# Attention products in halves, squares on ScalarE, tanh gates and a modulation plan in a two-layer encoder kernel

## The chip, the cores and the metric

The kernel runs as one program on one core of a Trainium2 chip. The metric is the device time of one execution in microseconds (us). Five engines matter: PE (TensorE, the matrix multiplier, with its weight loads listed as PEld), DVE (VectorE), ACT (ScalarE), POOL (GpSimd) and SP (SyncE, which here only issues transfers). Each engine takes its own instructions strictly in the order in which they stand; an instruction that waits holds up all behind it on its engine.

## The reference

Two layers, 256 tokens of width 2048, everything in float32. Each layer has an attention part and a feed-forward part, both behind a modulated norm:

```
mod = silu(c) @ ada_w[l] + ada_b[l]            # 6 rows of 2048: shifts, scales, gates
h   = rmsnorm(x) * (1 + sc_a) + sh_a
qa, ka, va, qb, kb, vb, ga, gb = split_cols(h @ w_in[l])
ya  = window_attention(rotary(norm(qa)), rotary(norm(ka)), va, sink) @ w_proj_a   # 8 heads, 2 of k and v
yb  = neighbourhood_attention(norm(qb), norm(kb), vb, bias) @ w_proj_b            # 8 heads
x   = x + gt_a * ((sigmoid(ga) * ya + sigmoid(gb) * yb) @ w_out)
h   = rmsnorm(x) * (1 + sc_m) + sh_m
g, v = split(conv3(h @ w_up))                  # 2 x 5632
x   = x + gt_m * ((silu(g) * v) @ w_down)
```

`norm` of q and k is an RMS norm over the 128 columns of a head. Attention is softmax(q k^T + mask or bias) v in both branches; branch A also has one sink logit per head in the softmax's sum.

## The kernel before, in words

**Products in halves.** A float32 matrix product is made of three products of the reduced type float32r. An operand is split into a high half (`hi`, a cast by ACT) and what is left over (`lo`, a subtraction by DVE), and PE adds hi·hi, hi·lo and lo·hi in PSUM. All weights go this way. They come in *units* of 16 blocks of 128x128 (1 MB, tile `w`), 232 units a layer, in the order in which PE needs them. For each unit ACT casts two halves of 128x1024 (`hl`, L296) and DVE subtracts (L297). There are four buffers for raw megabytes (weights `w` and modulation rows `aw` share them) and four for halves, so two units lie split ahead of PE. `features` multiplies activations of 256 tokens by a block (L313 to L315, 256 columns each); `tokens` makes rows of q, k and v (L373 to L375, 512 columns each).

**Attention before.** Only the products inside attention are done in plain float32: the scores `sc` (L570: two matmuls a head) and the outputs `po` (L601: two matmuls a head). The trace shows each float32 matmul as two records. Between them stand the mask with the row maximum (DVE, L574), the exponential (ACT, L582), the scaling (ACT, L590), four transposes (PE, `tp`, L595) and a copy of their result to SBUF (ACT, `pT`, L597). A head's output is itself split (`oA`, `oB`, L603 and L604). The heads run in a background job, several steps a unit (`ATT`), so their instructions lie between the weights' products.

**Norm of q and k** (`qk_rows`): for each of two token tiles ACT squares all heads' columns at once (L525), DVE sums each head's 128 columns (L526), a few small steps and a power on POOL (L420) give the factors, DVE multiplies (L534), and PE turns the result (`qtp`, L558).

**Gates.** Branch A's gate is `ya` (L864, in the second layer's start L735), branch B's is `gb` (L889), both a sigmoid on ACT. DVE multiplies the projected branches by them (L875 and L901) and the sum is split for the next product (L903).

**Modulation** (`ada`). Each of 96 columns of 128 values a layer is one transfer of 1 MB and one long DVE reduction (L225). In the first layer, while the first q, k and v groups are made, a job (`job0`) alternates two such reductions with one chunk of `h` (L445, L448, L449); its pace is `FIRST_RATE`, steps a unit. Afterwards `ADA_PLAN_0` and `ADA_PLAN_1` say how many reductions are done by which unit.

**Order.** The program text gives instructions priorities; a list scheduler that works with its own costs then fixes the order on each engine. All transfers are issued by SP in one order.

## Time and profile before

| | |
|---|---|
| three timed runs | 2687.84, 2690.78 (median), 2696.68 us |
| the profiled execution | 2687.88 us; its span on the core 2686.1 us, so 1.8 us lie around the span |
| busy: PE, DVE, ACT | 2663.7, 2086.4, 1402.2 us |
| transfers | 700 MB, 70.9% of the 16 DMA engines' time |

A busy PE is PE with a matmul in flight; matmuls overlap, so the mean duration of one (276 to 283 ns for 256 columns) is longer than the distance between two starts. Distances are therefore read from starts, or from a count of matmuls in a stretch where PE never idles. "Granted clock" (PEclk) is the share of full speed at which PE may run.

### The profile page before, as it was taken

The page shows a single profiled execution, that of the slowest core. Times are in us where ns is not written, and L with a number is a line of the kernel's source. Part 1 is how long each engine was busy: PE and PEld are TensorE (multiplying, and loading weights), DVE is VectorE, ACT ScalarE, POOL GpSimd, SP SyncE. Part 2 cuts the span into 40 slices and gives each one's busy share as a digit, 9 for nine tenths or more (in the row PEclk, how much of TensorE's full clock was granted, in tenths as well). Part 3 has the DMA queues.
Part 4 walks back from the last instruction along what each step waited for, and adds up shares of the span by engine and source line. Part 5 has one row for each costly group of instructions (what it writes and reads, how often), then busy time and mean ns, then how long its engine had stood idle before and what let it go on. Part 6 is the DMA issues. An engine that isn't in the chain of part 4 may idle for free.

```text
span 2686.1 us, 50251 instructions
## 1 busy us (share of the span) xinstructions
PE 2663.7 (99%) x21128; PEld 2568.6 (96%) x21128; DVE 2086.4 (78%) x2909; ACT 1402.2 (52%) x2077; POOL 33.8 (1%) x25
## 2 busy tenths in 40 slices
PE   8999999999999999999999999999999999999999
PEld 6988799999999999999998889999999999999999
DVE  7998997897987888788886666658878866665664
ACT  4434674455653555355564556544565445544553
POOL 0000100000000000000000000000000000000000
PEclk9999999999999999999999999999999999999999
DMA  8987688886788888778756656676747765555554
GB/s 345 348 330 280 242 300 328 332 313 221 282 288 291 294 290 295 297 285 295 288 213 243 249 210 226 224 265 254 291 171 289 295 252 191 197 193 191 194 197 142
DMA packets 102036, 700.38 MB, mean 261 GB/s; under 512 B 12721, under 2 KB 15025, under 8 KB 17969
## 3 DMA queue, kind: packets, MB, share of 16 engines
q1 hardware_dynamic: 101810, 697.17, 70.9%
q8 instruction: 165, 2.70, 0.4%
q14 instruction: 61, 0.50, 0.0%
HBM read 695.03 MB, written 2.10 MB: 260 GB/s over the span
## 4 chain that ended last, share of the span: by engine, by line
PE 88%; DVE 6%; DMA 3%; issue 2%; ACT 1%; POOL 1%; DVEq 0%; ACTq 0%; POOLq 0%
PE ps L313 24%; PE ps L315 24%; PE ps L314 24%; PE ps_t L374 4%; PE ps_t L375 4%; PE ps_t L373 4%; DMA aw<-in_aw 3%; DVE hl L297 2%; DVE aw L225 1%; PE po L601 1%; PE sc L570 1%; ACT hl L296 1%; POOL qrs L420 1%; PE tp L595 1%; DVE qn L534 0%
## 5 line engine op out<-in xcount | busy, mean ns | idle before, releaser
L297 DVE TENSOR_TENSOR hl<-w,hl 128x1024 fp32r<-128x1024 f32 x928 | 1129.5, 1223 | 366.6 <-ACT hl L296 364.8
L296 ACT CAST hl<-w 128x1024 fp32r<-128x1024 f32 x928 | 970.5, 1049 | 737.1 <-PE ps L315 478.0
L313 PE MATMUL ps<-h,hl 128*128 128x256 f32 x3328 | 923.3, 278 | 0.2 <-ACT hl L296 0.2
L314 PE MATMUL ps<-h,hl 128*128 128x256 f32 x3328 | 920.0, 277 | 0.0
L315 PE MATMUL ps<-h,hl 128*128 128x256 f32 x3328 | 919.8, 277 | 0.0
L313 PEld LDWEIGHTS ps<-h,hl 128*128 128x128 f32 x3328 | 624.8, 188 | 1.2 <-ACT hl L296 0.6
L314 PEld LDWEIGHTS ps<-h,hl 128*128 128x128 f32 x3328 | 625.3, 188 | 0.4
L315 PEld LDWEIGHTS ps<-h,hl 128*128 128x128 f32 x3328 | 624.3, 188 | 0.1
L225 DVE CUSTOM_DVE_ANT_0 aw<-aw,cact,ab 128x2048 f32<-128x2048 f32 x189 | 443.8, 2349 | 61.7 <-DMA aw<-in_aw 60.9
L373 PE MATMUL ps_t<-hl,h 128*128 128x512 f32 x576 | 227.2, 398 | 6.9 <-ACT h L448 3.6
L374 PE MATMUL ps_t<-hl,h 128*128 128x512 f32 x576 | 226.7, 394 | 0.9 <-DVE hl L297 0.8
L375 PE MATMUL ps_t<-hl,h 128*128 128x512 f32 x576 | 226.2, 394 | 0.0
L937 DVE SCALAR_TENSOR_TENSOR u<-ps,cw,u 128x255 f32<-128x255 f32 x304 | 146.4, 482 | 67.5 <-ACT u L935 63.5
L935 ACT ACTIVATE u<-ps,cw 128x256 f32<-128x256 f32 x152 | 85.7, 564 | 179.2 <-PE ps L315 179.1
L315 PE MATMUL ps<-merged,hl 128*128 128x256 f32 x512 | 142.0, 278 | 0.4 <-DVE hl L297 0.4
L313 PE MATMUL ps<-merged,hl 128*128 128x256 f32 x512 | 141.8, 278 | 0.5 <-DVE m L901 0.5
L314 PE MATMUL ps<-merged,hl 128*128 128x256 f32 x512 | 141.8, 277 | 0.0
L314 PE MATMUL ps<-act_o,hl 128*128 128x256 f32 x512 | 141.4, 276 | 0.0
L315 PE MATMUL ps<-act_o,hl 128*128 128x256 f32 x512 | 141.3, 276 | 0.0
L313 PE MATMUL ps<-act_o,hl 128*128 128x256 f32 x512 | 141.2, 276 | 0.0
L373 PEld LDWEIGHTS ps_t<-hl,h 128*128 128x128 f32 x576 | 108.8, 189 | 31.0 <-ACT h L448 4.6
L374 PEld LDWEIGHTS ps_t<-hl,h 128*128 128x128 f32 x576 | 109.2, 190 | 24.5 <-DVE hl L297 1.9
(215 smaller groups left out, 4562.2 us busy)
## 6 DMA issues: line engine op xcount, KB each, us to landing
w<-in_ws SPq DMA_DIRECT2D x463, 1024.0 KB, 5.0
aw<-in_aw SPq DMA_DIRECT2D x189, 1024.0 KB, 6.0
bias<-in_bias SPq DMA_DIRECT2D x16, 256.0 KB, 5.1
x<-in_xT SPq DMA_DIRECT2D x4, 512.0 KB, 5.3
aw_o<-in_aw SPq DMA_DIRECT2D x2, 1024.0 KB, 12.7
out<-x SPq DMA_DIRECT2D x16, 128.0 KB, 2.6
w<-in_ws SPq DMA_DIRECT2D x2, 512.0 KB, 12.1
aw_b<-in_aw SPq DMA_DIRECT2D x1, 1024.0 KB, 17.4
```

What stands on the lines that cost most here:

```text
L225: nc.vector.tensor_tensor_reduce(out=raw[:], in0=raw[:], in1=cact[:], scale=1.0, scalar=ab[:, i : i + 1], op0=ALU.mult, op1=ALU.add, accum ...
L296: nc.scalar.copy(hl[:, 0], r)
L297: nc.vector.tensor_tensor(out=hl[:, 1], in0=r, in1=hl[:, 0].bitcast(F32), op=ALU.subtract)
L313: nc.tensor.matmul(out, hi, act[0], start=first, stop=False)
L314: nc.tensor.matmul(ps[:, :S], hi, act[1], start=False, stop=False)
L315: nc.tensor.matmul(out, lo, act[0], start=False, stop=last)
L373: nc.tensor.matmul(ps[:], xh, hi, start=kc == kcs[0], stop=False)
L374: nc.tensor.matmul(ps[:], xh, lo, start=False, stop=False)
L375: nc.tensor.matmul(ps[:], xl, hi, start=False, stop=kc == kcs[-1])
L420: nc.gpsimd.tensor_tensor(out=dst, in0=src, in1=mhalf[:, :k], op=ALU.pow)
L935: nc.scalar.activation(out=u, in_=ps, func=AF.Identity, scale=w[:, 1:2], bias=w[:, 3:4])
L937: nc.vector.scalar_tensor_tensor(out=u[:, to], in0=ps[:, of], scalar=w[:, j : j + 1], in1=u[:, to], op0=ALU.mult, op1=ALU.add)
```

## The change

Six things are done together.

1. `attend` takes its operands as tuples. Where an operand comes as (hi, lo), the product is made of three float32r products (`by`). The outputs `po` go this way in both layers, the scores only in the second (`SCORES_3 = (1,)`). For this `pT` is split as it leaves PSUM (ACT cast and DVE subtraction of 512 columns in place of one ACT copy), v is split once per key head (2 in branch A, 8 in branch B), and in the second layer q (16), kA (2) and kB (8) are split too, 256 columns each.
2. `qk_rows`: ACT squares each head's 128 columns apart and sums them itself (`accum_out`), 52 instructions a layer in place of 14; the DVE sums L526 are gone.
3. Gates: sigmoid(z) = (1 + tanh(z/2)) / 2. ACT computes the tanh (same count of instructions); DVE multiplies by (1 + t) with one three-operand instruction in place of a product, and the factor 1/2 goes into the split of the merged sum.
4. The first layer's job follows `FIRST_PLAN`, steps done by a unit on straight lines, in place of rates.
5. Sixteen small matmuls of no use (`warm(WARM_ROW)`) stand behind the first chunk's products.
6. Buffers: the bias of branch B lands in the tile `p` itself; the small per-layer tables have one buffer in place of two, so the second layer's load later; sizes of fill-ins are adjusted.

```diff
-FIRST_RATE = [1.2, 1.0, 1.0]
+FIRST_PLAN = [(0, 6), (10, 17), (42, 48)]
+WARM_ROW = 16
+SCORES_3 = (1,)
...
+            if self.l == 0:
+                while ran[0] < on_line(FIRST_PLAN, self.u, True):
+                    first_step()
...
+                if self.l == 0 and self.u == 1 and self.at == 4:
+                    warm(WARM_ROW)
...
+        nc.scalar.activation(out=dst[:, 0], in_=src, func=AF.Copy, scale=scale)
+        nc.vector.scalar_tensor_tensor(
+            out=dst[:, 1], in0=src, scalar=scale, in1=dst[:, 0].bitcast(F32), op0=ALU.mult, op1=ALU.subtract
+        )
+    def half_tanh(dst, src, **kw):
+        nc.scalar.activation(out=dst, in_=src, func=AF.Tanh, scale=0.5, **kw)
+    def gated(dst, half, src):
+        nc.vector.scalar_tensor_tensor(out=dst, in0=half, scalar=1.0, in1=src, op0=ALU.add, op1=ALU.mult)
...
-            sq = at.tile([P, 512], F32, name="qsq", tag="qsq", bufs=1)
-            nc.scalar.activation(out=sq[:, :n], in_=ps[:, cols : cols + n], func=AF.Square)
-            nc.vector.tensor_reduce(
-                out=ss[:, t * heads : (t + 1) * heads], in_=sq[:, :n].rearrange("p (h d) -> p h d", d=HEAD), axis=AX.X, op=ALU.add
-            )
+            for i in range(heads):
+                sq = at.tile([P, HEAD], F32, name="qsq", tag="qsq", bufs=1)
+                nc.scalar.activation(
+                    out=sq[:], in_=ps[:, cols + i * HEAD : cols + (i + 1) * HEAD], func=AF.Square,
+                    accum_out=ss[:, t * heads + i : t * heads + i + 1],
+                )
...
+    def by(x):
+        return ((0, 0), (0, 1), (1, 0))[: 2 * len(x) - 1]
...
-            nc.tensor.matmul(sc[:, t], qT[:, t * P : (t + 1) * P], kT, start=True, stop=True)
+            for i, j in by(q):
+                nc.tensor.matmul(sc[:, t], q[i][:, t * P : (t + 1) * P], k[j], start=i + j == 0, stop=(i, j) == by(q)[-1])
...
-        pT = at.tile([P, 2, S], F32, name="pT", tag="pT", bufs=1)
-        nc.scalar.copy(pT[:], tp[:])
+        pT = at.tile([P, 2, 2, S], F32R, name="pT", tag="pT", bufs=1)
+        split(pT, tp[:])
...
-        for k in range(2):
-            nc.tensor.matmul(po[:, :S], v(k), pT[:, k], start=k == 0, stop=k == 1)
+        for i, j in by(v):
+            for b in range(2):
+                nc.tensor.matmul(po[:, :S], v[i][:, b], pT[:, j, b], start=i + j + b == 0, stop=i + b == 2)
...
-            bias = at.tile([P, 2, S], F32, name="bias", tag="bias", bufs=1)
-            nc.sync.dma_start(bias[:], a["bias"][l, hb])
+            p = at.tile([P, 2, S], F32, name="p", tag="p")
+            nc.sync.dma_start(p[:], a["bias"][l, hb])
...
-                split(merged[mo], z[:])
+                split(merged[mo], z[:], 0.5)
```

How the order moves is shown at three places. In its rows the numbers behind a name are layer-internal buffer numbers; `hl_2_0` is the first half of unit 2.

**DVE near the start of the first layer**, from the modulation row `aw_b` on. Before:

```order
L225 ISA aw_b_264,mod_172<-aw_b_264,cact,ab_173 128x2048
L225 ISA mod_172 128x1
L297 TENSOR_TENSOR hl_2_0_273<-w_2_271,hl_2_0_273 128x1024
L297 TENSOR_TENSOR hl_2_1_276<-w_2_271,hl_2_1_276 128x1024
L225 ISA aw_5_293,mod_172<-aw_5_293,cact,ab_173 128x2048
L225 ISA mod_172 128x1
L232 SCALAR_TENSOR_TENSOR amod_177<-mod_172,nrm_175 128x1
L445 SCALAR_TENSOR_TENSOR ht<-x,amod_177,rbs 128x256
L225 ISA aw_6_315,mod_172<-aw_6_315,cact,ab_173 128x2048
```

The same place in the changed kernel:

```order
L226 ISA aw_b_281,mod_172<-aw_b_281,cact,ab_173 128x2048
L226 ISA mod_172 128x1
L226 ISA aw_5_284,mod_172<-aw_5_284,cact,ab_173 128x2048
L226 ISA mod_172 128x1
L233 SCALAR_TENSOR_TENSOR amod_177<-mod_172,nrm_175 128x1
L466 SCALAR_TENSOR_TENSOR ht<-x,amod_177,rbs 128x256
L470 SCALAR_TENSOR_TENSOR h_0_171<-ht,mod_172,h_0_171 128x256
L298 TENSOR_TENSOR hl_2_0_294<-w_2_292,hl_2_0_294 128x1024
L298 TENSOR_TENSOR hl_2_1_297<-w_2_292,hl_2_1_297 128x1024
```

The reduction of `aw_5` and the third chunk of `h` that needs it now stand ahead of unit 2's split; the transfers of `aw_5` and of unit 2 have changed places on SP in the same way.

**PE in one head of branch A, first layer.** Before:

```order
L595 MATMUL tp<-ident,p 128x128 x3
L570 MATMUL sc<-packA_223 128x256
L315 MATMUL ps_50_6_0_2959<-h_0_171,hl_49_0_2855 128x256
L313 MATMUL ps_50_6_0_2959<-h_0_171,hl_49_0_2855 128x256
L314 MATMUL ps_50_6_0_2959<-h_0_171,hl_49_0_2855 128x256
L601 MATMUL po<-pT,packA_223 128x256 x2
```

In the changed kernel:

```order
L631 MATMUL tp<-ident,p 128x128 x3
L607 MATMUL sc<-packA_223 128x256
L316 MATMUL ps_50_6_0_3079<-h_0_171,hl_49_0_2961 128x256
L314 MATMUL ps_50_6_0_3079<-h_0_171,hl_49_0_2961 128x256
L315 MATMUL ps_50_6_0_3079<-h_0_171,hl_49_0_2961 128x256
L316 MATMUL ps_50_6_0_3079<-h_0_171,hl_49_0_2961 128x256
L314 MATMUL ps_50_6_0_3079<-h_0_171,hl_49_1_2964 128x256
L639 MATMUL po<-pT,vA_1_2807 128x256 x2
L315 MATMUL ps_50_6_0_3079<-h_0_171,hl_49_1_2964 128x256
```

Five weight products, not three, stand between the transposes and the first two output products; the other four output products, two of which need the low half of `pT` from DVE, follow five weight products later.

**ACT in the same stretch.** Before:

```order
L864 ACT_TABLE_LOAD
L864 ACTIVATE ya_222<-ya_222 128x256
L590 ACTIVATE p<-p,ri 128x256 x2
L864 ACTIVATE ya_222<-ya_222 128x256 x3
L597 COPY pT<-tp 128x512
L864 ACTIVATE ya_222<-ya_222 128x256 x2
L296 CAST hl_52_0_3283<-w_52_3281 128x1024
L603 CAST oA_6_2733<-po 128x256
L296 CAST hl_52_1_3286<-w_52_3281 128x1024
L582 ACT_TABLE_LOAD
L582 ACTIVATE p,den<-p,nm 128x256 x2
```

In the changed kernel:

```order
L618 ACTIVATE p,den<-p,nm 128x256 x2
L621 ACTIVATE es<-nm,sink_996 128x2
L399 ACTIVATE ya_222<-ya_222 128x256
L626 ACTIVATE p<-p,ri 128x256 x2
L399 ACTIVATE ya_222<-ya_222 128x256 x3
L389 CAST pT<-tp 128x512
L297 CAST hl_52_1_3434<-w_52_3429 128x1024
```

The table loads between exponentials and gates are gone. In the whole program 24 such loads become 5: one at the start, and in each layer one ahead of the first exponential and one ahead of the first silu.

104 lines of the change are left out of this document (62 added, 42 removed).

## The prediction

> **What bounds the kernel now.** I read the busy shares first, then the busy time by stretches, then the chain of waits.
>
> ```profile
> span 2686.1 us, 50251 instructions
> PE 2663.7 (99%) x21128; PEld 2568.6 (96%) x21128; DVE 2086.4 (78%) x2909; ACT 1402.2 (52%) x2077; POOL 33.8 (1%) x25
> 20.00:40.00 20.00, 15.74 (x56) 11.73 (x56) 15.43 (x16) 8.75 (x12) 0.00 (x0) 0.83 0.85 343
> 40.00:60.00 20.00, 17.00 (x64) 12.62 (x64) 16.85 (x21) 10.31 (x15) 0.00 (x0) 0.91 0.90 345
> 250.00:420.00 170.00, 164.79 (x1048) 145.91 (x1047) 154.92 (x302) 117.49 (x227) 14.65 (x6) 1.00 0.73 271
> 280.00:380.00 100.00, 97.66 (x619) 85.75 (x618) 96.39 (x199) 78.06 (x158) 6.92 (x4) 1.00 0.73 270
> 340.00:360.00 20.00, 19.50 (x145) 17.99 (x144) 19.11 (x46) 18.66 (x39) 0.00 (x0) 1.00 0.69 249
> 540.00:560.00 20.00, 19.50 (x167) 19.30 (x166) 19.50 (x39) 10.69 (x22) 0.00 (x0) 1.00 0.85 319
> 1000.00:1300.00 300.00, 300.00 (x2640) 300.00 (x2639) 249.19 (x320) 148.79 (x201) 0.00 (x0) 1.00 0.80 292
> 1460.00:1850.00 390.00, 388.62 (x2638) 357.59 (x2637) 255.73 (x380) 217.13 (x337) 11.58 (x6) 1.00 0.64 233
> ```
>
> The columns of a stretch are its length, busy PE, PEld, DVE, ACT and POOL, granted clock, DMA share and GB/s. PE is busy 99%, so only what takes work from PE, gives it back its clock, or fills the 22 us in which it is idle (2686.1 - 2663.7), can shorten the run. Three places differ from the rest. From 20 to 60 us PE is idle 7.3 us and its clock is granted at 0.83 and 0.91. From 280 to 380 us, the first layer's attention, DVE is busy 96.4 of 100 us: there DVE sets the pace with PE. In the second layer's attention (1460 to 1850) DVE is busy 66% and ACT 56%: there PE alone decides.
>
> **The products.** The chain of waits shows what two float32 matmuls cost while PE is saturated, first in the first layer, then in the second (start, length, records):
>
> ```profile
> 370.69 0.90 PE po L601 x4
> 377.74 1.02 PE po L601 x4
> 1507.09 0.86 PE sc L570 x4
> 1537.46 0.86 PE po L601 x4
> ```
>
> A pair takes 0.86 us. Six float32r products of 256 columns take 6 x 300/2640 = 0.68 us by the stretch from 1000 to 1300. So each replaced pair saves 0.18 us: 16 scores and 16 outputs in the second layer, 5.8 us; 16 outputs in the first, 2.9 us.
>
> **What the splits add.** Rows of the groups by line and form, mean ns before the bar that gives idle time:
>
> ```profile
> L526 DVE TENSOR_REDUCE qss<-qsq 128x4 f32<-128x512 f32 x24 | 16.4, 682 | 2.6 <-ACT qsq L525 2.3
> L526 DVE TENSOR_REDUCE qss<-qsq 128x2 f32<-128x256 f32 x4 | 1.7, 413 | 0.4 <-ACT qsq L525 0.4
> L831 DVE TENSOR_TENSOR packB<-ps_t,packB 128x512 f32<-128x512 f32 x24 | 16.2, 686 | 2.6 <-PE ps_t L375 2.5
> L382 DVE TENSOR_TENSOR merged<-m,merged 128x256 fp32r<-128x256 f32 x32 | 13.1, 420 | 0.2
> L937 DVE SCALAR_TENSOR_TENSOR u<-ps,cw,u 128x255 f32<-128x255 f32 x304 | 146.4, 482 | 67.5 <-ACT u L935 63.5
> L381 ACT CAST merged<-m 128x256 fp32r<-128x256 f32 x32 | 13.0, 405 | 18.3 <-DVE m L902 18.1
> L525 ACT ACTIVATE qsq<-ps_t 128x512 f32<-128x512 f32 x12 | 7.1, 592 | 4.1 <-PE ps_t L375 4.0
> L582 ACT ACTIVATION_READ_ACCUMULATOR p<-p,nm 128x1 f32 x64 | 12.0, 188 | 0.0
> L514 ACT ACTIVATE lsh<-ps 128x2 f32<-128x2 f32 x32 | 5.3, 167 | 15.2 <-PE ps L315 14.5
> L582 ACT ACT_TABLE_LOAD x10 | 12.8, 1283 | 0.2
> ```
>
> DVE, first layer's attention: the low half of `pT` is a 512-column subtraction from PSUM, like L831, 16 x 0.69 = 11.0 us; v's low halves 10 x 0.42 = 4.2; 16 gate products on `ya` at 0.48 in place of 0.42, 1.0; the sums that go, 12 x 0.68 + 2 x 0.41 = 9.0. Together +7.2 us. The second layer has 26 splits of q and k more: +10.9, so +18 us, against 134 us in which DVE is idle there. At the merge of each layer, 16 gate products and 16 scaled subtractions cost 0.06 more each, 1.9 us; in the first layer DVE is 97% busy at that place (540 to 560).
>
> ACT: a 128-column square with its sum is not in the trace. It lies between L514's 0.167 us (2 columns) and L525's 0.592 (512 columns), each with 0.188 for the read of the sum, so 0.36 to 0.78. I take 0.47, near the short end since 128 columns are a quarter of L525's. 52 of them are 24.4 us a layer, in place of 8.0 now (14 of L525, twelve at about 0.6 and two of half the columns). 19 table loads go, 7 in the first layer (-9.0 us) and 12 in the second (-15.4). With the casts of v, q and k (0.405 each) ACT gets 11 us more work in the first layer and 16 in the second (a tanh is taken to last as long as the sigmoid). Its idle time hides that: 31% of 250 to 420 and 44% of 1460 to 1850. If it did not, hl casts would come late and PE with them; two units of split weights (2 x 48 products, 11 us) stand between.
>
> *First layer.* 100 us of DVE's pace hold 3.6 us of idle time. If all 7.2 us fell there, DVE would end it 3.6 us later and PE's 2.9 us would be worth nothing: +4. If the sums that go relieve 240 to 300 us and the rest finds room behind 380, PE keeps its 2.9 us and loses some of its waits:
>
> ```profile
> PE qtp L558 <- DVE qn L551: 4.2, 3, 1.8
> PE tp L595 <- ACT p L590: 1.8, 3, 1.1
> ```
>
> That is at best -6 with about half of these 6 us. DVE is far nearer to full than to free, so I take +0.5, and +1.0 of 0 to 1.9 at the merge.
>
> *Second layer.* -5.8 us, less 1.0 for products that wait for a half just made: -4.8, ends -5.8 and -2 (a wait of 0.24 us in each of 16 heads).
>
> **The start.** Rows of the timeline:
>
> ```profile
> 20.37 0.63 PE L375 MATMUL ps_t<-hl,h 128*128 128x512 f32 x2
> 23.46 0.73 PE L373 MATMUL ps_t<-hl,h 128*128 128x512 f32 x2 [2.47 <-ACT hl L296]
> 25.99 0.79 PE L373 MATMUL ps_t<-hl,h 128*128 128x512 f32 x1 [1.79 <-ACT h L448]
> 27.57 0.63 PE L373 MATMUL ps_t<-hl,h 128*128 128x512 f32 x1
> 28.00 0.63 PE L374 MATMUL ps_t<-hl,h 128*128 128x512 f32 x1
> 34.27 0.39 PE L373 MATMUL ps_t<-hl,h 128*128 128x512 f32 x1
> 34.50 0.39 PE L374 MATMUL ps_t<-hl,h 128*128 128x512 f32 x1
> 36.03 2.36 DVE L297 TENSOR_TENSOR hl<-w,hl 128x1024 fp32r<-128x1024 f32 x2 [4.50 <-ACT hl L296]
> 38.31 2.35 DVE L225 CUSTOM_DVE_ANT_0 aw<-aw,cact,ab 128x2048 f32<-128x2048 f32 x1
> 41.98 0.51 PE L373 MATMUL ps_t<-hl,h 128*128 128x512 f32 x1 [1.29 <-ACT h L448]
> 46.23 0.50 PE L373 MATMUL ps_t<-hl,h 128*128 128x512 f32 x1 [0.91 <-ACT hl L296]
> 47.49 0.50 PE L374 MATMUL ps_t<-hl,h 128*128 128x512 f32 x1 [0.76 <-DVE hl L297]
> 16.96 1.50 PE L389 MATMUL warm<-ident 128*128 128x128 f32 x12
> ```
>
> After two waits (2.47 and 1.79) the starts lie 0.43 us apart (27.57, 28.00) in place of 0.23 (34.27, 34.50): PE runs at half clock for about 10 products, 2.0 us lost. Behind the waits at 42 to 47.5 the same happens for about 8, 1.5 us (the granted clock of 0.91 from 40 to 60 us). The waits there are 3.0 us. The new small products (12 took 1.50, so 16 take 1.8 to 2.0 at full clock) fit in the gap of 2.47; at half clock they would hold the next product back by about 1 us.
>
> DVE stood still for 4.5 us before 36.03 and made `aw_5`'s reduction only from 38.31, so the third chunk of `h` came at 41.9. With the reduction ahead of unit 2's split it can run in that idle time and the wait at 41.98 goes. The price is that unit 2's split follows it; PE, early by its kept clock, waits there up to 1 us. Of 6.5 us (2.0 + 1.5 + 3.0) I take 4.5, ends -6.5 and +1. Later the plan asks for fewer steps a unit (31 in 32 units in place of one each), which moves DVE's work by less than one reduction.
>
> The Trainium skill, in "TensorE: Matmul & The Clock Gate" (Part 1: The HAM clock gate), says that the clock falls after an idle window of about 3.4 us and that the windows run freely, so that the same kernel meets them in another phase each time. The trace agrees that it falls after idle time (0.83 granted where PE waits). By that rule the 16 small products keep the clock in some executions only, and the sum would lack up to 2.0 us in the others.
>
> **The small loads.** A head's bias lands in `p`, which is free only when the transposes of the head two before are done. Behind it on SP stand weight transfers.
>
> ```profile
> bias<-in_bias SPq DMA_DIRECT2D x16, 256.0 KB, 5.1
> ```
>
> Heads follow each other every 7.05 us in the first layer (370.69 to 377.74), so 5.1 us to landing leave 2: nothing is charged. If they did not, DVE's mask step would wait for each of 8 biases. The second layer's small tables (nrm, ab, gains, rg, sink) are now issued only when the first layer's have been read for the last time, with weights behind them on SP. Two units lie split ahead of PE (11 us), so nothing is charged; without that cover each of the five could cost PE one such landing.
>
> **The sum.** Start -4.5, first layer +0.5 +1.0, second layer -4.8: -7.8 us against the profiled execution's 2687.88, so 2680.1. That execution agrees with the fastest run of before (2687.84); the median is 2.9 above. I forecast 2680, 0.4% below the median.
>
> **The rivals.**
> 1. *The start's gain does not arrive* (0.17): transfers are 85 to 90% busy from 20 to 60 us, so weights come as before and PE only waits elsewhere. For it: the DMA share; against: DVE, not a transfer, released the waits at 42 to 47 us. 2680.1 + 4.5 = 2685.
> 2. *More than forecast* (0.20): the clock is kept, DVE finds room in the first layer and ACT without table loads (93% busy from 340 to 360) delivers `p` in time: -6.5 at the start, -5 of the best -6 in the first layer's attention, +0.5 at its merge, -5.8 = -17, 2671.
> 3. *The second layer's gain goes into waits* (0.11): each head's later products stand in PE's order where DVE is not ready; 2680.1 + 4.8 + 1 = 2686.
> 4. *Slower* (0.07): in the first layer the low half of `pT` comes late. PE has five products (0.57 us) between the first and the later output products, and the subtraction alone takes 0.69; if one split of weights (1.14, half of L297's 2.36 for two) stands ahead on DVE, PE waits 0.69 + 1.14 - 0.57 = 1.3 us a head, 20 us in 16 heads: 2700. It makes the kernel slower from (7.8 + 2.9)/16 = 0.7 us a head. Against it: the order keeps these products behind others, and DVE's waits are inside its own order.
>
> **How the numbers follow.** The forecast holds 0.45, with its own range 2675 to 2685. A difference under 0.3%, 8 us, cannot be told from none; the bound is 2682.7. Faster: three quarters of the forecast (0.34), rival 2 (0.20) and a quarter of rival 1 (0.04), 0.58. Slower: rival 4 nearly alone, 0.06. The rest, 0.36. The range 2671 to 2691 leaves out rival 4 and the far half of rival 2.
>
> **What would show it.** Right: distances of 0.68 us for six products; the clock at 1.00 from 20 to 40 us and no PE wait at 42 us; DVE above 96% from 280 to 380 us without longer PE waits; five table loads. Wrong: PE waits ahead of the later output products; PE waits on `hl` or `w` before 100 us that were not there; or a PE idle time above 22 us.

## The result and the profile after

| | median us | range us | executions |
|---|---|---|---|
| kernel before, on the same chip | 2690.02 | 2685.76 to 2697.88 | 6 |
| changed kernel | 2676.46 | 2671.69 to 2678.99 | 6 |

The ratio is 0.9944, with a 95% interval from 0.9932 to 0.9956: the change makes the kernel 0.56% faster, 13.6 us between the medians. The profiled execution took 2676.32 us, 11.6 less than the profiled one of before (2687.88).

From the page of the changed kernel, the span and the busy time of each engine; then its busy time by stretches, with the columns of the prediction's table (length, PE, PEld, DVE, ACT, POOL, granted clock, DMA share, GB/s):

```profile
span 2674.5 us, 50837 instructions
PE 2654.3 (99%) x21256; PEld 2565.6 (96%) x21256; DVE 2101.5 (79%) x2959; ACT 1409.0 (53%) x2284; POOL 33.3 (1%) x25
```

```profile
20.00:40.00 20.00, 17.99 (x92) 14.35 (x91) 18.37 (x20) 11.27 (x17) 0.00 (x0) 1.00 0.98 396
40.00:60.00 20.00, 19.63 (x84) 15.13 (x82) 17.80 (x22) 11.39 (x17) 0.00 (x0) 1.00 0.96 366
250.00:420.00 170.00, 163.90 (x1116) 147.56 (x1114) 160.55 (x312) 119.46 (x301) 11.95 (x5) 1.00 0.73 272
1460.00:1850.00 390.00, 389.74 (x2786) 363.63 (x2785) 275.21 (x438) 223.16 (x437) 8.18 (x5) 1.00 0.63 238
```

PE has gained 2.3 us from 20 to 40 and 2.6 us from 40 to 60, at full clock. From 250 to 420 us PE, DVE and ACT look much as before. In the second layer's attention DVE carries 20 us more and PE is idle for 0.3 of 390 us.

**Where the 11.6 us came from.** PE makes its weight products in a fixed sequence, 48 of 256 columns a unit (a product of 512 columns counts twice). So the starts of the products in the trace can be counted, and the start of a unit's first product is a mark that means the same work in every kernel here. Two marks stand in rows of the products by tile (durations in ns, then the first and the last start in us): the first product of `oA` opens unit 52, the first of `merged` unit 84. Before, then the changed kernel:

```profile
L313 PE MATMUL ps<-oA,hl x256: 275/277/470, 347.9 to 1731.0; 128*128 128x256 f32 x128
L313 PE MATMUL ps<-merged,hl x512: 274/276/384, 546.4 to 1956.8; 128*128 128x256 f32 x171
```

```profile
L314 PE MATMUL ps<-oA,hl x256: 276/277/387, 342.6 to 1721.0; 128*128 128x256 f32 x128
L314 PE MATMUL ps<-merged,hl x512: 274/276/384, 539.6 to 1945.2; 128*128 128x256 f32 x171
```

The first layer's `oA` starts 5.3 us earlier, its `merged` 6.8 us, and the second layer's last `merged` product 11.6 us. The table has the same count for the whole run, with a second profiled execution of the changed kernel (told below) beside the first:

| stretch (units) | before, us | changed | second execution | forecast | found |
|---|---|---|---|---|---|
| start (to 40) | 254.5 | 249.1 | 249.3 | -4.5 | -5.3, -5.1 |
| first layer's attention (40 to 62) | 171.7 | 170.2 | 169.7 | +0.5 | -1.5, -2.0 |
| merge and after (62 to 104) | 234.7 | 232.9 | 233.7 | +1.0 | -1.8, -1.0 |
| rest of the first layer (104 to 244) | 771.2 | 776.0 | 771.2 | 0 | +4.7, 0.0 |
| second layer's attention (244 to 312) | 415.7 | 407.9 | 407.8 | -4.8 | -7.8, -7.9 |
| to the last unit (312 to 463) | 829.4 | 829.4 | 829.4 | 0 | 0.0, 0.0 |

The sums are -11.6 and -16.0 us, where -7.8 was forecast. The first execution lies nearer to the forecast only because it lost 4.7 us in a stretch that the change leaves as it is.

### The profile page after: what moved, and what is told of

Its sections match the earlier page's. It is cut to its first block, busy times and chain, and to the rows that moved or that the text cites. A ratio compares the mean times of both kernels' runs of the same rounds, so it can differ in the third digit from the quotient of the medians.

```text
span 2674.5 us, 50837 instructions
## 1 busy us (share of the span) xinstructions
PE 2654.3 (99%) x21256; PEld 2565.6 (96%) x21256; DVE 2101.5 (79%) x2959; ACT 1409.0 (53%) x2284; POOL 33.3 (1%) x25
## 4 chain that ended last, share of the span: by engine, by line
PE 84%; DMA 6%; DVE 6%; issue 2%; ACT 1%; POOL 0%; SPq 0%; DVEq 0%; ACTq 0%; POOLq 0%
PE ps L314 23%; PE ps L316 23%; PE ps L315 23%; DMA aw<-in_aw 5%; PE ps_t L378 4%; PE ps_t L377 4%; PE ps_t L379 4%; DVE hl L298 2%; DVE aw L226 2%; PE po L639 1%; PE sc L607 1%; DMA w<-in_ws 1%; ACT hl L297 1%; PE tp L631 1%; POOL qrs L441 0%
## 5 line engine op out<-in xcount | busy, mean ns | idle before, releaser
L377 PE MATMUL ps_t<-hl,h 128*128 128x512 f32 x576 | 223.4, 393 | 2.8 <-ACT h L469 1.9
L378 PE MATMUL ps_t<-hl,h 128*128 128x512 f32 x576 | 225.1, 391 | 0.3
L379 PE MATMUL ps_t<-hl,h 128*128 128x512 f32 x576 | 224.6, 391 | 0.0
L989 ACT ACTIVATE u<-ps,cw 128x256 f32<-128x256 f32 x152 | 85.6, 563 | 164.3 <-PE ps L316 164.1
```

Source lines behind the costliest of these rows:

```text
L377: nc.tensor.matmul(ps[:], xh, hi, start=kc == kcs[0], stop=False)
L378: nc.tensor.matmul(ps[:], xh, lo, start=False, stop=False)
L379: nc.tensor.matmul(ps[:], xl, hi, start=False, stop=kc == kcs[-1])
L989: nc.scalar.activation(out=u, in_=ps, func=AF.Identity, scale=w[:, 1:2], bias=w[:, 3:4])
```

## The experiments

Each kernel was run beside the kernel before on the same chip. The times of stretches are those of the table above, counted in the same way from each kernel's profiled execution. Two executions of the same kernel differ there by up to 0.8 us, apart from the 4.7 us that have a part of their own below. A stretch that a variant leaves as it is can be 1.0 us longer, since the order is made anew (the second layer's attention takes 408.8 us, not 407.8, in the variant that edits the first layer alone). Differences of that size are not read unless a wait accounts for them.

### The start: order or clock

**The first layer's plan alone** is the kernel before with `FIRST_PLAN` and nothing else:

```diff
-FIRST_RATE = [1.2, 1.0, 1.0]
+FIRST_PLAN = [(0, 6), (10, 17), (42, 48)]
...
+                while ran[0] < on_line(FIRST_PLAN, self.u, True):
+                    first_step()
```

> The kernel before with the line FIRST_PLAN in place of FIRST_RATE, nothing else. Before, the stretch from the first product of q, k and v (18.9 us) to the first product of oA (347.9) takes 329.0 us; in the changed kernel 324.0. Theory (DVE's new order makes the start's gain, the small products add nothing): 323.5 to 325, and the whole run 4 to 6 us faster. Rival (the kept clock makes it): 327 or more.

It took 2683.55 us, ratio 0.9984 (0.9974 to 0.9993). Unit 40 starts 4.3 us earlier and everything behind it keeps this (3.8 at the end). By the marks of the expectation it takes 324.8 us, so the theory held there and its rival fell. All waits of PE from 20 to 60 us (us in total, times, longest):

```profile
PE ps_t L376 <- ACT hl L296: 2.3, 1, 2.3
PE ps_t L376 <- ACT h L451: 2.0, 1, 2.0
```

The three waits between 41 and 48 us that the prediction showed are gone; the first two, ahead of 27 us, are still there, and so is the half clock behind them (granted 0.83 from 20 to 40). DVE's timeline in the changed kernel shows what moved:

```profile
31.37 2.35 DVE L226 CUSTOM_DVE_ANT_0 aw<-aw,cact,ab 128x2048 f32<-128x2048 f32 x1
...
35.01 0.48 DVE L470 SCALAR_TENSOR_TENSOR h<-ht,mod,h 128x256 fp32r<-128x256 f32 x1 [0.58 <-ACT h L469]
```

The row's reduction runs at 31.37, in time in which DVE had stood still until 36.03; the third chunk of `h` is written at 35.0 (the wait for it had ended at 41.98), and the split of unit 2 follows at 35.95, at the same time as before.

**The changed kernel without the sixteen small products:**

```diff
-WARM_ROW = 16
+WARM_ROW = 0
```

> The changed kernel without the sixteen small products (WARM_ROW 0), all else kept. Places are read from the first start of oA's products in the first layer, 342.6 us in the changed kernel. Theory (the kept clock is part of the start's gain): about ten products near 26 to 31 us are again 0.43 us apart, PE loses up to 2.0 us there, and since unit 2's split comes at 36 us, 0.5 to 2 us of it stay: first oA at 343 to 345, whole run +0.5 to +2 us. Rival (the order of DVE alone makes the gain): first oA at 342.6 within 0.3, the run unchanged.

It took 2674.37 us, ratio 0.9952 (0.9938 to 0.9967), as fast as the changed kernel. Its profiled execution began late for another reason: the twelve small products that fill PE's time from 14 us on, which both kernels have (24 records, since each float32 product is two), ran at half clock, and the products that spread the norm's factors (`rb`) stand behind them. Rows of PE's timeline, the changed kernel's first, then this one's:

```profile
13.42 2.92 PE L410 MATMUL warm<-ident 128*128 128x128 f32 x24
```

```profile
14.47 4.97 PE L410 MATMUL warm<-ident 128*128 128x128 f32 x24
...
28.52 0.50 PE L377 MATMUL ps_t<-hl,h 128*128 128x512 f32 x1 [3.85 <-ACT h L469]
```

Without the sixteen, PE waits 3.85 us, and the products behind run at half clock (0.63 us each and 0.43 from start to start). Yet from unit 0 to unit 4 it takes 29.6 us, the plan alone 30.1, the changed kernel 29.3 and 28.8, and before 35.5. So the order makes 5.5 of the 6.2 to 6.7 us and the sixteen products at most 1.2. From unit 0 to the first `oA` it takes 324.0 us, as the changed kernel does (324.0 and 323.0): the rival held. A PE that comes early at full clock meets the next `h` or `hl` and waits there. Two rows of the changed kernel show this. In the first are the sixteen small products, two records each; in the second PE waits for unit 2's half:

```profile
20.26 3.73 PE L410 MATMUL warm<-ident 128*128 128x128 f32 x32
...
35.97 1.20 PE L377 MATMUL ps_t<-hl,h 128*128 128x512 f32 x4 [0.99 <-ACT hl L297]
```

They take 3.73 us. The prediction took 1.8 to 2.0, because it read the 12 records of 1.50 us as twelve products; they are six. So they fill the gap of 2.47 us to its end and beyond.

### The products in halves

**Scores in plain float32 in both layers:**

```diff
-SCORES_3 = (1,)
+SCORES_3 = ()
```

> The changed kernel with the second layer's scores in plain float32 again (SCORES_3 empty; q and k are not split). From the first product of q, k and v to the first product of merged the second layer takes 451.6 us in the changed kernel and 459.4 before. Theory (PE sets this stretch, a float32 pair costs 0.17 us more than six products in halves, the late start of the product behind it included): 16 x 0.17 = 2.7 us, so 454.3. Rival (DVE or ACT sets it, 26 splits of 0.42 us fewer): 451.6 or less.

2674.87 us, ratio 0.9954 (0.9939 to 0.9969). The second layer's attention takes 410.9 us, 3.0 to 3.1 more than the changed kernel; the 16 score pairs in halves are worth that much, 0.19 us each. In the total this drowns: the median lies inside the changed kernel's range.

**Outputs in plain float32 in both layers,** so that `pT` and v are not split:

```diff
-        split(pT, tp[:])
+        nc.scalar.copy(pT[:], tp[:])
...
-        for i, j in by(v):
-            for b in range(2):
-                nc.tensor.matmul(po[:, :S], v[i][:, b], pT[:, j, b], start=i + j + b == 0, stop=i + b == 2)
+        for b in range(2):
+            nc.tensor.matmul(po[:, :S], v[0][:, b], pT[:, b], start=b == 0, stop=b == 1)
```

> The changed kernel with the outputs in plain float32 again (no split of v and pT); the second layer's scores stay in halves. PE gets 32 x 0.16 to 0.35 us more (the upper end if each pair also holds up the product behind it), DVE 15 us less a layer. Theory: second layer, from the first product of q, k and v to the first of merged, 451.6 + 2.5 to 5 = 454 to 457; first layer, where DVE sets the pace, no loss or a gain: last oA at 402 to 407. Rival (PE sets both layers): first layer as well 2.5 to 5 us later, last oA at 409 to 411.

2684.25 us, ratio 0.9987 (0.9978 to 0.9997). The second layer's attention takes 411.3 us, 3.4 to 3.5 more than the changed kernel (0.21 a pair). But the first layer's takes 176.9, 6.7 to 7.2 more, though 15.6 us of DVE's work are gone there. Neither theory nor rival has this: the last `oA` starts at 414.9. Its stretch; the longest of PE's waits between 245 and 425 us; then the two longest of the changed kernel:

```profile
250.00:420.00 170.00, 159.16 (x1025) 141.32 (x1024) 144.93 (x283) 114.36 (x287) 11.11 (x5) 1.00 0.72 261
```

```profile
PE tp L631 <- ACT p L626: 7.3, 6, 1.7
```

```profile
PE qtp L580 <- DVE qn L573: 3.5, 2, 1.8
PE tp L631 <- ACT p L626: 1.5, 1, 1.5
```

PE waits 7.3 us for softmax's `p` in place of 1.5. So less work on DVE did not make this stretch shorter. That the place of the heads' steps between PE's products decides is a guess: no run moved them and nothing else.

The products themselves are seen where PE never waits. The chain of waits of the changed kernel in the second layer (a head of branch A), and the same three steps of a head of branch B in the timeline of before:

```profile
1532.20 0.71 PE po L639 x6
1532.91 0.44 PE tp L631 x4
1533.34 0.70 PE sc L607 x6
```

```profile
1760.78 1.02 PE L601 MATMUL po<-pT,packB 128*128 128x256 f32 x4
...
1762.08 1.03 PE L570 MATMUL sc<-packB 128*128 128x256 f32 x4
1762.76 0.47 PE L313 MATMUL ps<-h,hl 128*128 128x256 f32 x1
1763.07 0.28 PE L314 MATMUL ps<-h,hl 128*128 128x256 f32 x1
```

In the changed kernel the head's block lasts 0.71 + 0.44 + 0.70 = 1.85 us. Before, it lasts from 1760.78 to 1763.07 less one product of 0.11, 2.18 us: the four score records start over 0.68 us, and the first weight product behind them then takes 0.31 to the next start where its followers take 0.11, so the pair costs 0.87. The saving is 0.33 us a head, 5.3 us in 16 heads.

**Scores in halves in the first layer too:**

```diff
-SCORES_3 = (1,)
+SCORES_3 = (0, 1)
```

> The changed kernel with the scores in halves in both layers. It adds 26 splits of 0.42 us on DVE and 0.41 on ACT (10.9 and 10.5 us) to the first layer's attention and takes 2.7 us from PE. The last product of oA starts at 406.4 us there in the changed kernel. Theory (DVE sets the first layer's attention): PE waits more than it saves, last oA at 410 to 415, whole run +3 to +9 us. Rival (PE sets it, DVE's high busy share is work that it does ahead): last oA at 403 to 404, run -2.7 us.

2679.12 us, ratio 0.9971 (0.9961 to 0.9981). The first layer's attention takes 173.6 us, 3.4 to 3.9 more than the changed kernel, though PE has some 2.6 us less to do. The three of PE's waits there that have grown most, one for ACT and two for DVE:

```profile
PE tp L631 <- ACT p L626: 3.8, 3, 1.5
PE ps L314 <- DVE hl L298: 2.6, 1, 2.6
PE ps L314 <- DVE ya L915: 2.2, 2, 1.3
```

The theory held in the time. But the 26 splits give ACT 10.5 us more and DVE 10.9, and the largest of these waits is for ACT's `p`, so the loss cannot be put down to DVE alone. More work on both does not fit there, while 15.6 us less on DVE did not help.

### Tanh and the squares

**Tanh alone,** the kernel before with the new gates:

```diff
-                        nc.scalar.activation(out=ya[:, mo], in_=src, func=AF.Sigmoid)
+                        half_tanh(ya[:, mo], src)
...
-                nc.vector.tensor_tensor(out=ya[:, mo], in0=ps, in1=ya[:, mo], op=ALU.mult)
+                gated(ya[:, mo], ya[:, mo], ps)
...
-                split(merged[mo], z[:])
+                split(merged[mo], z[:], 0.5)
```

> The kernel before with the gates by tanh alone (24 table loads become 5; 32 DVE products a layer cost 0.06 us more). First oA 347.9 to last oA 414.8 us before: 66.9. Theory (PE waits in the first layer's attention for the softmax on ACT, so a freer ACT helps): 64 to 66; second layer from the first product of q, k and v to the first of merged 459.4 within 0.7. Rival (ACT's idle time hides table loads): 66.9 within 0.5, and 1 to 2 us lost at the first layer's merge, where DVE is 97% busy.

2685.76 us, ratio 0.9990 (0.9980 to 0.9999). The first layer's attention is 2.2 us shorter (169.5), the second layer's not at all (415.7), though more table loads went there. From first to last `oA` it takes 63.4 us, a little less than the theory had.

**The accumulated squares alone,** the kernel before with the new `qk_rows`:

```diff
-            nc.scalar.activation(out=sq[:, :n], in_=ps[:, cols : cols + n], func=AF.Square)
-            nc.vector.tensor_reduce(
+            for i in range(heads):
+                nc.scalar.activation(..., func=AF.Square, accum_out=ss[:, t * heads + i : t * heads + i + 1])
```

> The kernel before with q's and k's squares summed by ScalarE alone: DVE 9 us less a layer, ACT 16 us more. Rows: ps_t's first start to oA's last in the first layer, 18.9 to 414.8 us before. Theory (the softmax on ACT sets PE's waits there, not DVE's load): 0 to 3 us later. Rival (DVE's load sets the pace): 3 us or more earlier. Second layer, first product of q, k and v to first of merged, 459.4 before: both expect 0 to 1.5 us less, since the wait of 1.5 us for qn at 1465 us may go.

2703.01 us, ratio 1.0055 (1.0040 to 1.0070), the one part that is plainly slower by itself. The first layer's attention takes 189.6 us, 18 more; the last `oA` comes 17 us later, where the theory had 0 to 3 and the rival a gain. The 20 us in which PE is idle longest; PE's longest wait from 245 to 425 us; the table loads from 250 to 420 us:

```profile
360.00:380.00 20.00, 14.21 (x73) 11.50 (x71) 8.35 (x22) 19.86 (x36) 0.00 (x0) 0.81 0.31 105
```

```profile
PE tp L596 <- ACT p L591: 12.9, 9, 3.2
```

```profile
L583 ACT ACT_TABLE_LOAD x7 | 9.0, 1283 | 0.1
L865 ACT ACT_TABLE_LOAD x6 | 7.7, 1283 | 0.1
```

ACT is full (19.86 of 20 us) and PE waits 12.9 us for `p`. PE's clock falls behind long waits (0.81 granted in that row): four times in this stretch the trace has half clock for 3.41 us. Exponentials and sigmoids alternate more often than before: 13 loads of 1.28 us in place of 8 in the kernel before. From this I formed a theory, that the squares pay only beside tanh, and two runs for it. It fell in both.

**Squares and tanh together** on the kernel before, both diffs above:

> The kernel before with the accumulated squares and the gates by tanh, and nothing else of the change. Theory (ScalarE is the tight engine of the first layer's attention: alone, the squares cost 17 us there, because they came to 13 more us of ScalarE and broke the grouping of exp with sigmoid, so that 13 table loads of 1.28 us stood in 250 to 420 us where 8 had stood): with tanh these loads fall to 1, the squares cost next to nothing, and the kernel is 1 to 4 us faster than the kernel before: the stretch of the first layer's attention within 2 us of the kernel with tanh alone, and 1 us gained in the second layer at the wait for qn. Rival (the accumulated squares are slow whatever stands beside them, by their own 0.31 + 0.19 us for each of 128 columns or by holding a PSUM bank longer): 8 to 15 us slower than the kernel before, with PE waiting over 8 us for p of ScalarE in 250 to 420 us.

2689.20 us, ratio 1.0007 (0.9998 to 1.0017): neither the theory's gain nor the rival's 8 to 15 us of loss. The first layer's attention takes 177.9 us, so tanh wins back 11.7 of the 18 us, and 6 stay. The first of the waits that stay begins in the timeline of DVE and POOL:

```profile
254.00 2.35 DVE L225 CUSTOM_DVE_ANT_0 aw<-aw,cact,ab 128x2048 f32<-128x2048 f32 x1 [3.03 <-DMA aw<-in_aw]
...
256.27 0.17 DVE L435 TENSOR_SCALAR qss<-qss 128x8 f32<-128x8 f32 x1
...
256.52 2.54 POOL L436 TENSOR_TENSOR qrs<-qss,mhalf 128x8 f32<-128x8 f32 x1 [15.76 <-DVE qss L435]
```

In this order the small step on `qss` stands behind a modulation row that landed 3 us late, though the last square was done at 253.9; PE waits 3.4 us at one place. The median of its executions, 2689.20, is 4.2 below the profiled one (2693.39), whose start was 2.1 us late besides, with the small products at half clock as above. Another 2 us of the 6 may therefore belong to that execution alone.

**The changed kernel with sigmoid gates,** the diff of tanh alone undone:

> The changed kernel with the gates by sigmoid, as before, and all else as changed. Theory (tanh pays for the squares and for the halves in the first layer): the first layer's attention 12 to 25 us slower than the changed kernel's, ScalarE over 85% busy in 250 to 420 us with more than 8 table loads there, PE waiting over 8 us for p of ScalarE; the start and the second layer as in the changed kernel, but for up to 2 us; in all 2688 to 2702 us, no better than the kernel before. Rival (VectorE sets the pace there, and has 0.3 us per gate less to do nowhere, so the form of the gate matters little): within 4 us of the changed kernel, 2673 to 2680 us.

2672.02 us, ratio 0.9942 (0.9925 to 0.9958): as fast as with tanh. Its stretch, and its table loads there:

```profile
250.00:420.00 170.00, 163.64 (x1111) 147.16 (x1110) 159.72 (x311) 128.60 (x306) 12.70 (x6) 1.00 0.73 269
```

```profile
L618 ACT ACT_TABLE_LOAD x4 | 5.1, 1283 | 0.1
L918 ACT ACT_TABLE_LOAD x3 | 3.8, 1283 | 0.1
L943 ACT ACT_TABLE_LOAD x1 | 1.3, 1283 | 0.0
```

Eight loads are back and ACT is busy 128.6 us, more than in the kernel that lost 18 us, and the attention still takes 170.3 us. In the order of the changed kernel ACT's work has room. So tanh does not pay for the squares, and ACT's amount of work, taken alone, does not explain these runs. The second layer's attention is 1.6 us longer than the changed kernel's (409.4): PE waits 1.1 us there for `p`, as it does not with tanh.

**The changed kernel with the squares' sums on DVE again,** 256 columns at a time:

```diff
-                nc.scalar.activation(
-                    out=sq[:], in_=ps[:, cols + i * HEAD : cols + (i + 1) * HEAD], func=AF.Square,
-                    accum_out=ss[:, t * heads + i : t * heads + i + 1],
-                )
+                nc.scalar.activation(out=sq[:], in_=ps[:, cols + i * HEAD : cols + (i + 2) * HEAD], func=AF.Square)
+                nc.vector.tensor_reduce(out=ss[:, t * heads + i : t * heads + i + 2], ..., axis=AX.X, op=ALU.add)
```

> The changed kernel with q's and k's squares summed by VectorE again, 256 columns at a time: 26 squares of ScalarE and 26 sums of VectorE a layer in place of 52 accumulating squares of ScalarE, in both layers. Theory (from two runs: the kernel before with squares and tanh loses 6.3 us between 254 and 424 us, the changed kernel with its outputs in plain float32 5.2 us; so the accumulated squares cost about 5 us in the first layer's attention whatever stands beside them, and the outputs in halves hide this in the changed kernel): the first layer's attention 4 to 7 us shorter than the changed kernel's, the second layer 1 us longer at the wait for qn; 2667 to 2671 us. Rival (once VectorE has the low halves of pT and v to make, it is the tight engine there, and the squares' 10.7 us of VectorE are exactly what it lacks): the first layer's attention 3 to 6 us longer, VectorE busy over 165 of the 170 us from 250 to 420, PE waiting over 4 us for halves (hl) or for pT made by VectorE; 2678 to 2683 us.

2679.31 us, ratio 0.9968 (0.9957 to 0.9980). The rival's time came true: the first layer's attention takes 175.6 us, 5.4 to 5.9 more, and PE waits for DVE at several places, of which these are the longest:

```profile
PE ps L314 <- DVE ya L916: 2.3, 2, 2.1
PE qtp L581 <- DVE qn L574: 2.2, 1, 2.2
```

Its two signs did not. PE waits for no `hl`, and 1.1 us for `pT`, where the rival had over 4. DVE's busy time from 250 to 420 us did not rise over 165 us (159.6): unit 62 starts at 425.6 us in place of 419.3, so part of the work now lies behind 420. Behind the wait for `qn` PE runs 3.41 us at half clock, which costs another 1.7. The second layer's attention takes 409.0 us, 1.1 to 1.2 more, because the wait for `qn` near 1465 us is back. PE's waits from 1455 to 1500 us, where the changed kernel waits 0.3 us:

```profile
PE qtp L581 <- DVE qn L574: 1.4, 1, 1.4
```

**Plain outputs and DVE's sums in the first layer alone,** the second as changed:

```diff
+            if l == 0:
+                sq = at.tile([P, 512], F32, name="qsq0", tag="qh", bufs=1)
+                nc.scalar.activation(out=sq[:, :n], in_=ps[:, cols : cols + n], func=AF.Square)
+                nc.vector.tensor_reduce(...)
+                continue
...
-        split(pT, tp[:])
+        if len(q) == 1:
+            nc.scalar.copy(pT[:, 0], tp[:])
+        else:
+            split(pT, tp[:])
```

> The changed kernel with its first layer's attention as before in two things: outputs in plain float32 without splits of pT and v, and squares summed by VectorE 512 columns at a time; tanh, the start's plan and all of the second layer as changed. Theory (in the first layer's attention the halves and the accumulated squares each lose alone, 4 to 6 us, and together only win that back, so what is left is tanh's 2 us): the stretch from 254 to 426 us of before is 2 us shorter, the same as in the changed kernel within 1 us; 2672 to 2677 us in all. Rival (the halves' 2.9 us of PE do arrive in the changed kernel, and the orders of the other runs lost for reasons of their own): 3 to 5 us longer than the changed kernel there, 2676 to 2681 us.

2675.65 us, ratio 0.9950 (0.9934 to 0.9967), the same as the changed kernel. The first layer's attention takes 171.2 us, 1.0 to 1.5 more. That is at the edge of the theory's "within 1 us" and far from the rival's 3 to 5. With it the table of that stretch is complete (in its lower left cell DVE sums 256 columns at a time, in the upper left 512):

| first layer's attention, tanh gates, us | squares summed by DVE | squares accumulated by ACT |
|---|---|---|
| outputs in float32 | 171.2 (169.5 in the order of before) | 176.9 (177.9 in the order of before) |
| outputs in halves | 175.6 | 170.2 and 169.7 |

Each of the two alone loses 4 to 8 us; together they end 1.0 to 1.5 us ahead of neither, or level with tanh alone. The lengths do not come out of a sum of parts.

The same profiles show which part of a length adds up. Between the starts of units 40 and 62 the next table takes away the time in which PE has no matmul in flight, and half of its busy time at half clock (by the trace's record of the granted clock). The rest is PE at work at full clock:

| first layer's attention, us | length | PE idle | lost to half clock | rest |
|---|---|---|---|---|
| kernel before | 171.7 | 5.2 | 0 | 166.5 |
| tanh alone | 169.5 | 4.3 | 0 | 165.2 |
| squares alone | 189.6 | 17.3 | 6.4 | 165.8 |
| squares and tanh | 177.9 | 9.7 | 1.7 | 166.5 |
| changed, outputs in float32 | 176.9 | 10.8 | 0 | 166.1 |
| changed, plain first layer | 171.2 | 3.6 | 1.7 | 165.8 |
| changed kernel, two executions | 170.2, 169.7 | 6.1, 5.8 | 0 | 164.1, 163.9 |
| changed, sigmoid gates | 170.3 | 6.4 | 0 | 163.9 |
| changed, DVE's sums | 175.6 | 9.9 | 1.7 | 164.1 |
| changed, scores in halves too | 173.6 | 11.2 | 0 | 162.4 |

The rest falls into three groups: outputs in float32, outputs in halves (about 2 us less), scores in halves too (1.5 to 1.7 less again). So PE's work does add up, whatever stands beside it. What does not add up is the waiting and the half clock behind some of the waits.

### The 4.7 us between 1180 and 1357 us

**The changed kernel once more,** with no edit:

> The changed kernel once more, word for word but for a comment. Its first profile lost 4.7 us between 1180 and 1357 us, where its order on DVE, ACT and SP is that of before and DVE waited 20 us for modulation rows. Theory (an event of that one execution): the span is 2669 to 2671 us and DVE waits there under 8 us. Rival (the changed kernel's own state at that place): the loss is there again, span 2674 us.

2673.01 us, ratio 0.9946 (0.9929 to 0.9962). The stretch from unit 104 to 244 takes 771.2 us, as before, not 776.0. What DVE waited for from 1180 to 1357 us, first in the first execution, then in this one:

```profile
DVE aw L226 <- DMA aw<-in_aw: 20.1, 14, 3.2
```

```profile
DVE aw L226 <- DMA aw<-in_aw: 6.0, 9, 1.2
```

In the first execution the modulation rows landed late, with the same instructions in the same order. All other profiles of this study have 771.2 to 772.6 us there. Why those rows were late is open; it belongs to that execution and not to the change.

## Why the prediction was right, and where its sum was not

The forecast of 2680 us (2671 to 2691) holds the median of 2676.46, and the direction was right. The sum was short: the medians lie 13.6 us apart, where the forecast was 7.8 below the profiled execution, and every one of its four terms came out better than forecast. That the median is still in the range owes something to the range's width. The terms:

**The start, forecast -4.5, found -5.1 to -5.3.** "With the reduction ahead of unit 2's split it can run in that idle time and the wait at 41.98 goes": the plan alone shows it, 4.3 us. The charge for unit 2's split, up to 1 us, was due: PE, early by its kept clock, waits there 0.99 us, in the second execution 0.52. So the 2.0 us for the kept clock are the part that was sized too high: the clock was kept (1.00 granted from 20 to 40 us) and by unit 4 the gain was 1.2 us at most. The sixteen products themselves were also misjudged, 3.73 us for 1.8 to 2.0; this cost little, since the next `h` came late anyway. The rule of the Trainium skill that the prediction weighed, in "TensorE: Matmul & The Clock Gate" (Part 1: The HAM clock gate), that the windows of the clock run freely, agrees with the trace: in each execution all changes of the granted clock between the first rise and the last fall lie whole multiples of 3.41 us apart (in the kernel before at 13.98, 24.22, 31.05, 48.11 and 51.53 us), and the first rise came at 12.57 to 19.05 us. The idle window of about 3.4 us that the prediction quotes with it is not the shortest wait that costs the clock here: it fell behind single waits of 2.24 us (sums on DVE) and 2.00 us (plain first layer). That the sixteen keep the clock in some executions only was not seen: it was 1.00 from 20 to 40 us in all eight profiled executions that have them.

**The first layer's attention, forecast +0.5, found -1.5 to -2.0.** The term was PE's -2.9 us and +3.4 for waits. PE's part arrived, at 2.4 to 2.6 us. The step that failed is the charge for waits, drawn from "there DVE sets the pace": PE's idle time grew by only 0.6 to 0.9 us, while DVE was busy 3.7 us more between the same marks. More splits do lose time (scores in both layers), and so do sums on DVE, but so does less of DVE's work (plain outputs with accumulated squares), and then PE waits for `p`. No price of one engine's work, laid beside the others', gave these waits. "Its idle time hides that" held for ACT in the changed kernel, and fell by 18 us when the squares stood alone. Rival 2's mechanism, that ACT without table loads delivers `p` in time, is not what happened: with the table loads put back, the stretch is as long. The prediction also misread one row: the 4.2 us in three waits for `qn` are those of the whole run. From 245 to 425 us there are two, 2.8 us, and the third, 1.4 us, is the second layer's.

**The merge, forecast +1.0, found -1.0 to -1.8.** The three-operand instructions were priced at 0.48 us after a row with other operands. They take no longer than the ones they replace, so the term should have been zero. Groups of the changed kernel (mean ns before the bar), then of the kernel before:

```profile
L403 DVE SCALAR_TENSOR_TENSOR ya<-ya,ps 128x256 f32<-128x256 f32 x32 | 13.2, 414 | 2.6 <-PE ps L316 2.6
L393 DVE SCALAR_TENSOR_TENSOR merged<-m,merged 128x256 fp32r<-128x256 f32 x32 | 13.2, 421 | 0.1
```

```profile
L875 DVE TENSOR_TENSOR ya<-ps,ya 128x256 f32<-128x256 f32 x32 | 13.4, 422 | 6.4 <-PE ps L315 6.4
```

Where the gain itself comes from is open. Squares and tanh together show 1.8 us here, tanh alone 0.1, squares alone 0.9, the plan alone none, and differences up to about 1 us are not read.

**The second layer, forecast -4.8, found -7.8.** Split as in the table above, PE's work fell by 6.7 us (414.3 to 407.6), where 5.8 was forecast, and its idle time by 1.1 (1.4 to 0.3). Taken out one at a time, scores and outputs cost 3.0 and 3.4 us, 6.4 together; the one head shown above gives 0.33 us where 0.36 was forecast, so it does not hold all of it. "Less 1.0 for products that wait for a half just made" was wrong: PE is idle 0.3 of 390 us. The 1.1 us are the third wait for `qn`, which stood behind the squares' sums on DVE; the prediction had its row, but counted it to the first layer.

**ACT's and DVE's new instructions** were sized right: a square of 128 columns with its sum was taken at 0.47 us, 24.4 us a layer. Half of them read PSUM and took 24.6 us by the first two groups of the changed kernel; the other 52 read SBUF (307 and 309 ns, and 187 for each sum) and took 25.7, so it was 25.2 a layer. The low half of `pT` took 0.685 us where 0.69 was taken:

```profile
L547 ACT ACTIVATE qsq<-ps_t 128x128 f32<-128x128 f32 x52 | 14.4, 276 | 5.3 <-PE ps_t L379 4.2
L547 ACT ACTIVATION_READ_ACCUMULATOR qsq<-ps_t 128x1 f32 x52 | 10.2, 196 | 0.0
L390 DVE TENSOR_TENSOR pT<-tp,pT 128x512 fp32r<-128x512 f32 x32 | 21.9, 685 | 1.9 <-ACT pT L389 1.9
```

**The rivals.** The start's gain arrived (rival 1 fell); the second layer's gain did not go into waits (rival 3 fell). A late low half of `pT` (rival 4) was seen ahead of the outputs only as 0.2 us in the changed kernel, 0.5 with sigmoid gates and 0.6 with sums on DVE, at one place each. Rival 2 was near in its time (2671; the second execution took 2671.91) but not in its parts: the start and the first layer gave less than it had, the merge and the second layer more. Of the signs named beforehand for a right forecast, the clock, the wait at 42 us, the five table loads and DVE's share (96.0 and 96.3% from 280 to 380 us) came; one sign of a wrong one came too, the new wait for unit 2's `hl`. What was near to slower is not a single late half but an order in which one part stands without the other: the squares alone were 15 us slower than before.

**What stays open.** That PE's work adds up in the first layer's attention and its waits do not is shown, by one or two profiled executions of each kernel. Why each order gives the waits that it gives was seen at single places only (the row ahead of `qss`, the alternation of exponentials and sigmoids). Order and amount of work change together whenever a part is taken out, since the scheduler makes the order anew, and no run held the one fixed.

None of the variants is measurably faster than the changed kernel: those with sigmoid gates (2672.02), without the small products (2674.37), with plain scores (2674.87) and with a plain first layer (2675.65) have intervals that overlap its own two (ratios 0.9932 to 0.9956 and 0.9929 to 0.9962).

## What to carry to other kernels

Where one engine alone is saturated and the others have slack, as in the second layer here, a count of instructions by their measured distance predicts well: 5.8 us forecast, 6.7 found. Where three engines are all near full and a scheduler fixes the order, sum the parts of the work but not the waits: split each stretch into work, idle time and half clock, and try the parts together and in pairs, because two edits that each lose 4 to 8 us can be level or ahead together. A wait that another wait follows is worth little by itself; take the one for the operand that is made latest, here by moving one reduction into idle time ahead of a split that could wait.

## What the runs showed of the hardware

- A float32 pair of 256 columns ahead of float32r products costs 0.68 us in its own starts and 0.19 us at the first product behind it (0.31 to the next start in place of 0.11). Six float32r products cost 0.70 to 0.71 with no such tail.
- A three-operand instruction of DVE on 256 columns (0.414 and 0.421 us) took no longer than the two-operand one (0.422).
- An accumulating square of 128 columns took 0.28 us out of PSUM and 0.31 out of SBUF, and 0.19 us more for the read of its sum: for so few columns that read is two fifths of the cost.
- PE's clock was lost behind a single wait. In the changed kernel with sums on DVE, PE had worked without a stop, waited 2.24 us, and then ran seven products at 0.43 us from start to start in place of 0.23. Behind 1.81 us at the same place in the kernel before it kept its clock. The clock changed only at times that lie whole multiples of 3.41 us apart within an execution, so how long a wait may be could hang on where it falls; no run shows the least length. PE's timeline, the former and the latter:

```profile
257.15 1.31 PE L581 MATMUL qtp<-ident,qn 128*128 128x128 f32 x8 [2.24 <-DVE qn L574]
...
259.53 0.63 PE L377 MATMUL ps_t<-hl,h 128*128 128x512 f32 x1
```

```profile
261.64 1.06 PE L558 MATMUL qtp<-ident,qn 128*128 128x128 f32 x8 [1.81 <-DVE qn L551]
...
263.25 0.39 PE L375 MATMUL ps_t<-hl,h 128*128 128x512 f32 x1
```

- Small products that are to keep the clock can run at half clock themselves and hold up what stands behind them: twelve of them (24 records) took 4.97 us in place of 2.92, and unit 0 started 2.1 to 2.9 us later.
